# A state-space stage with its group norms, splits, weight copies and convolution banks placed elsewhere

## The chip, the cores and the metric

The kernel runs on one core of one Trainium2 chip. The metric is the device time of one execution in microseconds (us). TensorE (PE) multiplies 128x128 tiles, VectorE (DVE), ScalarE (ACT) and GpSimd (POOL) work element by element, and SyncE (SP) issues the transfers. Each engine runs its own list of instructions strictly in order and waits on semaphores for the others.

## What is computed

A two-layer trunk over 512 rows of 1024 numbers. The change lies in the first layer's mixer, a Mamba-2 state-space layer with four groups of eight heads, cut here to what matters:

```python
proj = h @ w_in
z, xbc, dt = split(proj)
xbc = silu(causal_dwconv(xbc, conv_w, conv_b))     # 4 taps
xs, bm, cm = split(xbc)
y = ssd_scan(xs, bm, cm, dt, dt_bias, a_log)       # two chunks of 256 rows
y = (y + d_skip * xs) * silu(z)
y = rmsnorm(y in 4 groups of 512, norm_g)          # a norm for each group
return y @ w_out
```

## The kernel before

All large products are made from operands that are split into a high and a low part (`split`: ACT copies the high part, DVE subtracts it for the low part), so each 128x128x512 step is three matmuls (`mm3`: lines 153, 154 and 155; `mm3_rows`: lines 387 to 389). Weights come in units of 128x1024 numbers, eight steps each: SP loads a unit into one of four `raw` buffers, and `split_unit` turns it into two of the six `w` buffers, so three units can be ready. `Weights.next` gives out the parts of the current unit in order; `prefetch` loads and splits a unit ahead.

`mamba` goes through four groups g. For each it makes six products (`linear`, 24 matmuls each: the state's B and C, and four of x), each followed by `conv` (one ACT instruction, three on DVE that read the accumulator bank) and a Silu on ACT. Then `ssd` makes the group's scan: it loads the heads' decay exponents (`exponents`: an SP transfer and two POOL additions for each head), and goes through four pairs of heads j: exponentials on ACT (line 824), a product with the shared matrix on DVE (825), matmuls (831, 835, 838), the skip and sum on DVE (843, 845), a gate (`gate`: one more `linear` of 24 matmuls, and a Silu, line 754), a product with it on DVE (847), a square on ACT (849) and its sum over the pairs in `ssq` on DVE (851). At its end comes the group's norm: `rstd` (eight small matmuls, line 319, that sum `ssq` over partitions, a chain of some ten small DVE instructions, lines 297 to 310, and four transposes, line 323), and four DVE multiplications by it (855).

In the code `split_group(g - 1)` follows the scan of group g: four copies on ACT and four subtractions on DVE that make `xo`, the operands of the output projection (`project_out`, which in its first part goes through 16 steps k of 12 matmuls each, with one `mod`, a load and two DVE instructions, in each). In group 0 three of the four gates are made before the scan.

Of the eight PSUM banks two are named `acc`, four `seg` and two `mi`. In groups 1 to 3 the six products and the gates take the two `acc` banks in turn; a bank comes free when the conv's third DVE instruction, or the gate's Silu, has read it. The pool `b4` has 33 buffers of 128x1024 numbers; `h`, `xo`, the exponent tiles, a group's u, xd, y and others all live there.

The order on each engine is fixed when the program is built. A planner takes, for an engine that it believes idle, the ready instruction that stands first in the code; so work that is written later can fill gaps, and where two instructions could run, the one written first does. Buffers of a pool are given out in the same way.

Of the kernel before, what the change touches and what calls it, by code (L numbers as in the profile page):

```python
# [13 lines left out]
AF = mybir.ActivationFunctionType  # L14
OP = mybir.AluOpType
# [9 lines left out]
KI = DI // P  # L25
# [67 lines left out]
class Kernel:  # L93
# [294 lines left out]
        nc.tensor.matmul(ps, x[0][:, ts], wl, start=False, stop=False)  # L388
        nc.tensor.matmul(ps, x[1][:, ts], wh, start=False, stop=stop)  # L389

    def project_out(self, dram, x, x_src, gain, x_dst, first=None, after=None, mods=(), held=()):

        nc = self.nc
        nk = len(x)
        row = self.rows(gain)
        sq = self.small.tile([P, 2, 4], F32, name="sq")
        yg = [None] * 4
# [10 lines left out]
        if first is not None:  # L410
            cols = [1]
            weights = Weights(self, dram)
            pss = first
            for k in range(nk):
                wh, wl = weights.next(4)
                for t in range(4):
                    self.mm3_rows(pss[t], x[k], t, wh, wl, k == 0, k == nk - 1)
                if k < len(mods):
                    self.mod(mods[k])
            for t in range(4):  # L420
                evacuate(pss[t], t, 0)
        xin = self.load_x(x_src)
        held = list(held)
        for i in range(2):
# [25 lines left out]
            for part in ([t] for t in ts) if after is None else [ts]:  # L450
# [3 lines left out]
                rs = self.rsqrt(s, D)  # L454
                for t in part:
                    for cs in [slice(0, D)] if after is not None else [slice(0, 512), slice(512, D)]:
                        nc.vector.scalar_tensor_tensor(out=xin[t][:, cs], in0=yg[t][:, cs], scalar=rs[:, t - lo:t - lo + 1],
                                                       in1=xin[t][:, cs], op0=OP.mult, op1=OP.add)
# [224 lines left out]
    def mamba(self, x, x_src, x_dst):  # L683
        nc = self.nc
        with ExitStack() as es:
            self.keep = es.enter_context(self.tc.tile_pool(name="ssm", bufs=1))
            c = self.constants(CST_M, "cst_m")
            w = Weights(self, self.a["ssm_in"])
            xn = [self.big((P, D)) for _ in range(4)]
            self.unit_rows(x, xn)  # L690
            h = self.pairs(KD)
            scale = self.const.tile([P, KD], F32, name="sc_first")
            pss = self.banks(6)
            for k in range(KD):
# [5 lines left out]
                for n in range(6):  # L700
                    wh, wl = w.next()
                    self.mm3(pss[n], wh, wl, h[k][0], h[k][1], k == 0, k == KD - 1)
            yn, xo = [], []

            def split_group(g):
                for u in yn[g]:
                    m = self.big(dt=F32R)
                    self.split(m[:, 0], m[:, 1], u)
                    xo.append((m[:, 0], m[:, 1]))

            mods = range(16, 24)
            for g in range(4):
# [24 lines left out]
                        zs.append(self.gate(w, h, z[1][:, 0], self.seg()))  # L737
                else:
                    for i in range(6):
                        nc.scalar.activation(u[i], self.conv(self.linear(w, h), tiles[i]), AF.Silu)  # L740
                for j in mods[MODS_SSM[g]:MODS_SSM[g + 1]]:
                    self.mod(j)
                yn.append(self.ssd(g, u[0], u[1], u[2:], w, h, c, zs))
                if g:
                    split_group(g - 1)
            split_group(3)
            gain = self.scale_cols(("post_mix", 0), 16, 0.0)
            h, after = self.before(("pre_ffn", 0), 24)
            self.project_out(self.a["ssm_out"], xo, x_src, gain, x_dst, self.banks(4), after, range(24, 40))
        return h  # L750

    def gate(self, w, h, out, ps=None):
# [14 lines left out]
        nc.gpsimd.tensor_tensor(out=v[:, :, 0], in0=v[:, :, 0], in1=mask, op=OP.add)  # L767
        return e

    def ssd(self, g, bt, ct, xs, w, h, c, zs):  # L770

        nc = self.nc
        es = [self.exponents(8 * g + i, c) for i in range(2)]
# [43 lines left out]
        for j in range(4):  # L817
            mh = []
            now = es
            es = [self.exponents(8 * g + 2 * j + 2 + i, c) for i in range(2)] if j < 3 else []  # L820
            for i, m in enumerate(now):
                hd = 8 * g + 2 * j + i
                for at, n, b in ((0, 256, 0), (256, 256, 2), (512, 128, 1), (640, 128, 3)):
                    nc.scalar.activation(m[:, at:at + n], m[:, at:at + n], AF.Exp, bias=self.nacs[:, b, hd:hd + 1])
                nc.vector.tensor_tensor(out=m, in0=m, in1=cb, op=OP.mult)
                mh.append(m)
# [23 lines left out]
            if j:  # L850
                nc.vector.tensor_tensor(out=ssq, in0=ssq, in1=sq, op=OP.add)
            out.append(y)
        rs = self.rstd(ssq, 512)
        for j in range(4):
            nc.vector.scalar_tensor_tensor(out=out[j], in0=out[j], scalar=self.col("ssm_norm", 4 * g + j), in1=rs,
                                           op0=OP.mult, op1=OP.mult)
        return out


    def rope(self, ps, factor, flat, out):  # L860
# [481 lines left out]
```

## Time and profile before

| | us |
|---|---|
| median of three runs | 1537.9 |
| lowest and highest | 1534.82, 1541.6 |
| the profiled execution | 1535.77 |
| its span, first to last instruction | 1534.0 |

The stretch that the change touches is 86 to 403 us of the span: group 0's scan ends near 121, those of groups 1, 2 and 3 near 192, 273 and 357 us, and the output projection's first part ends at 402. PE's clock has two levels, 2.4 and 1.2 GHz, shown as 1.00 and 0.50 in the column PEclk.

### The profile page before, as it was taken

The page shows a single profiled execution, that of the slowest core. Times are in us where ns is not written, and L with a number is a line of the kernel's source. Part 1 is how long each engine was busy: PE and PEld are TensorE (multiplying, and loading weights), DVE is VectorE, ACT ScalarE, POOL GpSimd, SP SyncE. Part 2 cuts the span into 40 slices and gives each one's busy share as a digit, 9 for nine tenths or more (in the row PEclk, how much of TensorE's full clock was granted, in tenths as well). Part 3 has the DMA queues.
Part 4 walks back from the last instruction along what each step waited for, and adds up shares of the span by engine and source line. Part 5 has one row for each costly group of instructions (what it writes and reads, how often), then busy time and mean ns, then how long its engine had stood idle before and what let it go on. Part 6 is the DMA issues. An engine that isn't in the chain of part 4 may idle for free.

```text
span 1534.0 us, 22547 instructions
## 1 busy us (share of the span) xinstructions
PE 1467.8 (96%) x8514; PEld 1217.7 (79%) x8514; DVE 1112.4 (73%) x1989; ACT 764.8 (50%) x1360; POOL 196.1 (13%) x161
## 2 busy tenths in 40 slices
PE   6999899898999999999999989999999999999997
PEld 4767677676889788888888877777678999999886
DVE  7877676787585788872367588889856878888246
ACT  3574839384363222322257474566644455557143
POOL 0040203040000000000000100000000356661000
PEclk9999999999999999999999999999999999999999
DMA  8443253454763788882466542000043223323254
GB/s 298 164 140 101 65 167 95 151 178 159 261 218 103 270 310 291 294 281 97 163 218 229 125 164 69 15 29 15 15 151 137 70 84 111 109 98 110 97 206 151
DMA packets 70687, 230.47 MB, mean 150 GB/s; under 512 B 8209, under 2 KB 11793, under 8 KB 70578
## 3 DMA queue, kind: packets, MB, share of 16 engines
q1 hardware_dynamic: 70290, 228.77, 44.3%
q8 instruction: 67, 1.10, 0.3%
q14 instruction: 42, 0.34, 0.1%
q10 hardware_dynamic: 288, 0.25, 0.1%
HBM read 215.30 MB, written 8.45 MB: 146 GB/s over the span
## 4 chain that ended last, share of the span: by engine, by line
PE 76%; DVE 13%; DMA 4%; ACT 3%; issue 2%; SPq 1%; POOL 0%; DVEq 0%; ACTq 0%
PE acc L153 12%; PE acc L154 12%; PE acc L155 12%; PE seg L389 5%; PE seg L388 5%; PE seg L387 5%; PE seg L155 3%; PE seg L154 3%; PE seg L153 3%; PE acc L388 3%; PE acc L389 3%; PE acc L387 3%; DVE w L134 2%; PE mi L1190 2%; PE acc L1207 2%
## 5 line engine op out<-in xcount | busy, mean ns | idle before, releaser
L134 DVE TENSOR_TENSOR w<-raw,w 128x1024 fp32r<-128x1024 f32 (+1 forms) x250 | 308.4, 1240 | 180.4 <-ACT w L133 173.3
L133 ACT ACTIVATE w<-raw 128x1024 fp32r<-128x1024 f32 (+1 forms) x250 | 242.2, 971 | 388.0 <-PE seg L388 124.6
L153 PE MATMUL acc<-b,w 128*128 128x512 f32 (+1 forms) x976 | 360.4, 370 | 11.0 <-ACT w L133 6.3
L155 PE MATMUL acc<-b,w 128*128 128x512 f32 (+1 forms) x976 | 356.6, 365 | 0.5 <-DVE w L134 0.5
L154 PE MATMUL acc<-b,w 128*128 128x512 f32 (+1 forms) x976 | 355.4, 364 | 0.5 <-DVE b L134 0.5
L153 PEld LDWEIGHTS acc<-b,w 128*128 128x128 f32 x976 | 186.0, 191 | 42.8 <-ACT w L133 7.0
L155 PEld LDWEIGHTS acc<-b,w 128*128 128x128 f32 x976 | 186.2, 191 | 29.2 <-DVE w L134 1.0
L154 PEld LDWEIGHTS acc<-b,w 128*128 128x128 f32 x976 | 186.2, 191 | 27.6 <-DVE b L134 1.3
L271 DVE SCALAR_TENSOR_TENSOR raw<-raw,b 128x1024 f32<-128x1024 f32 x112 | 136.1, 1221 | 27.5 <-DMA raw<-in_mod_dram 26.8
L388 PE MATMUL seg<-w,b 128*128 128x512 f32 x340 | 133.0, 391 | 0.0
L389 PE MATMUL seg<-w,b 128*128 128x512 f32 x340 | 133.0, 391 | 0.0
L387 PE MATMUL seg<-w,b 128*128 128x512 f32 x340 | 132.7, 391 | 0.0
L867 POOL TENSOR_TENSOR t<-t,b 128x512 f32<-128x512 f32 x12 | 18.0, 1499 | 717.0 <-DVE t L866 714.1
L1158 ACT ACTIVATE b<-seg,nm 128x512 f32<-128x512 f32 (+3 forms) x128 | 65.9, 525 | 64.1 <-DVE nm L1155 63.3
L155 PE MATMUL seg<-b,w 128*128 128x256 f32 (+1 forms) x252 | 77.2, 306 | 1.4 <-DVE w L134 1.4
L154 PE MATMUL seg<-b,w 128*128 128x256 f32 (+1 forms) x252 | 77.1, 306 | 0.0
L153 PE MATMUL seg<-b,w 128*128 128x256 f32 (+1 forms) x252 | 75.6, 306 | 0.0
L389 PEld LDWEIGHTS seg<-w,b 128*128 128x128 f32 x340 | 64.1, 189 | 13.3
L388 PEld LDWEIGHTS seg<-w,b 128*128 128x128 f32 x340 | 64.1, 189 | 13.3
L387 PEld LDWEIGHTS seg<-w,b 128*128 128x128 f32 x340 | 63.8, 188 | 13.0
L133 ACT ACTIVATE b<-t 128x256 fp32r<-128x256 f32 (+1 forms) x94 | 46.3, 516 | 48.9 <-DVE t L539 30.3
L134 DVE TENSOR_TENSOR w<-st,w 128x512 fp32r<-128x512 f32 x68 | 56.9, 841 | 18.6 <-ACT w L133 15.9
(309 smaller groups left out, 2846.4 us busy)
## 6 DMA issues: line engine op xcount, KB each, us to landing
raw<-in_mod_dram SPq DMA_DIRECT2D x112, 512.0 KB, 4.6
raw<-in_ffn_in_dram SPq DMA_DIRECT2D x88, 512.0 KB, 4.2
raw<-in_ffn_out_dram SPq DMA_DIRECT2D x66, 512.0 KB, 3.3
raw<-in_ssm_in_dram SPq DMA_DIRECT2D x41, 512.0 KB, 4.3
raw<-in_ssm_out_dram SPq DMA_DIRECT2D x24, 512.0 KB, 4.2
b<-acsd SPq DMA_DIRECT2D x40, 256.0 KB, 5.2
raw<-in_kv_dram SPq DMA_DIRECT2D x12, 512.0 KB, 4.4
raw<-in_q_dram SPq DMA_DIRECT2D x9, 512.0 KB, 4.6
```

The lines of the kernel that those rows point to most:

```text
L133: nc.scalar.activation(hi, src, AF.Copy)
L134: nc.vector.tensor_tensor(out=lo, in0=src, in1=hi.bitcast(F32), op=OP.subtract)
L153: nc.tensor.matmul(ps, wh, xh, start=start, stop=False, skip_group_check=more)
L154: nc.tensor.matmul(ps, wh, xl, start=False, stop=False, skip_group_check=more)
L155: nc.tensor.matmul(ps, wl, xh, start=False, stop=stop, skip_group_check=more)
L271: i = nc.vector.scalar_tensor_tensor(out=raw, in0=raw, scalar=1.0, in1=self.cs, op0=OP.mult, op1=OP.mult, accum_out=self.modc[:, n:n + 1])
L387: nc.tensor.matmul(ps, x[0][:, ts], wh, start=start, stop=False)
L388: nc.tensor.matmul(ps, x[0][:, ts], wl, start=False, stop=False)
L389: nc.tensor.matmul(ps, x[1][:, ts], wh, start=False, stop=stop)
L1158: nc.scalar.activation(p[o + r], banks[i][:, r * n:(r + 1) * n], AF.Exp, bias=nm[:, o + r:o + r + 1], accum_out=d[:, o + r:o + r + 1])
L1190: nc.tensor.transpose(ps[:, i * n + a * P:i * n + (a + 1) * P], unit["p"][j * per + i][:, a * P:(a + 1) * P], self.ident)
L1207: self.nc.tensor.matmul(po[64 * i:64 * i + 64, bs], vt[a][:, r * 256 + kv * 64:r * 256 + kv * 64 + 64], unit["w"][2 * i + r][:, a * P:(a + ...
```

## The change

- `ssd` no longer ends with its norm. It returns the norm as a function `end`. In groups 1 to 3 the end of group g - 1 is called after the first of group g's six products; that of group 3 is called in `project_out` at step k = 2.
- `split_group` becomes `split_two`. Group g - 1 is split within group g's projections, two tiles after the fifth convolution and two after the sixth; group 3's tiles are split in `project_out` at k = 6. So xo of group g - 1 exists before the scan of group g, and no longer after it.
- In `ssd`, before the exponentials of the last pair (j = 3), three units of weights are asked for: that of the last gate, and two for the next group's first products (none of these two in group 3).
- The six products of groups 1 to 3 go to the four `seg` banks in turn; the gates keep the `acc` banks.

```diff
-    def project_out(self, dram, x, x_src, gain, x_dst, first=None, after=None, mods=(), held=()):
+    def project_out(self, dram, x, x_src, gain, x_dst, first=None, after=None, mods=(), held=(), nk=None, at=None):
-        nk = len(x)
+        nk = nk or len(x)
...
                 wh, wl = weights.next(4)
+                if at is not None and k in at:
+                    at[k]()
                 for t in range(4):
...
-            def split_group(g):
-                for u in yn[g]:
+            def split_two(g, i):
+                for u in yn[g][2 * i:2 * i + 2]:
...
-                        nc.scalar.activation(u[i], self.conv(self.linear(w, h), tiles[i]), AF.Silu)
+                        ps = self.linear(w, h, self.seg())
+                        if i == 0:
+                            ends.pop()()
+                        nc.scalar.activation(u[i], self.conv(ps, tiles[i]), AF.Silu)
+                        if i > 3:
+                            split_two(g - 1, i - 4)
...
-                yn.append(self.ssd(g, u[0], u[1], u[2:], w, h, c, zs))
-                if g:
-                    split_group(g - 1)
-            split_group(3)
+                out, end = self.ssd(g, u[0], u[1], u[2:], w, h, c, zs, 2 if g < 3 else 0)
+                yn.append(out)
+                ends.append(end)
+
+            def last():
+                split_two(3, 0)
+                split_two(3, 1)
...
-            self.project_out(self.a["ssm_out"], xo, x_src, gain, x_dst, self.banks(4), after, range(24, 40))
+            self.project_out(self.a["ssm_out"], xo, x_src, gain, x_dst, self.banks(4), after, range(24, 40), nk=KI,
+                             at={2: ends.pop(), 6: last})
...
+            if j == 3:
+                if not zs[j:]:
+                    w.prefetch()
+                for _ in range(ahead):
+                    w.prefetch()
...
-        rs = self.rstd(ssq, 512)
-        for j in range(4):
-            nc.vector.scalar_tensor_tensor(out=out[j], in0=out[j], scalar=self.col("ssm_norm", 4 * g + j), in1=rs,
-                                           op0=OP.mult, op1=OP.mult)
-        return out
+
+        def end():
+            rs = self.rstd(ssq, 512)
+            for j in range(4):
+                nc.vector.scalar_tensor_tensor(out=out[j], in0=out[j], scalar=self.col("ssm_norm", 4 * g + j), in1=rs,
+                                               op0=OP.mult, op1=OP.mult)
+
+        return out, end
```

## Rows read from the trace of the kernel before

**Rows 1.** The page's first part: busy us, share of the span, instructions.
```profile
PE 1467.8 (96%) x8514; PEld 1217.7 (79%) x8514; DVE 1112.4 (73%) x1989; ACT 764.8 (50%) x1360; POOL 196.1 (13%) x161
```
**Rows 2.** Busy time by stretch: from:to, length, each engine's busy time, PEclk, DMA.
```profile
20.00:40.00 20.00, 20.00 (x84) 15.95 (x83) 18.51 (x42) 5.63 (x8) 0.00 (x0) 1.00 0.90 294
...
99.50:118.40 18.90, 14.64 (x81) 9.06 (x79) 18.54 (x24) 13.44 (x29) 9.89 (x9) 1.00 0.12 42
...
150.00:184.00 34.00, 33.82 (x174) 24.43 (x174) 23.27 (x33) 30.72 (x53) 13.60 (x16) 1.00 0.34 98
184.00:192.00 8.00, 3.92 (x23) 1.90 (x21) 6.57 (x12) 7.25 (x12) 0.00 (x0) 1.00 0.00 0
192.00:198.80 6.80, 6.80 (x20) 5.74 (x21) 4.90 (x14) 0.63 (x1) 0.00 (x0) 0.50 0.57 185
...
208.10:230.40 22.30, 22.19 (x97) 18.09 (x98) 17.02 (x26) 8.88 (x14) 0.00 (x0) 1.00 0.62 196
...
273.90:280.70 6.80, 6.80 (x20) 5.54 (x20) 4.50 (x14) 0.25 (x1) 0.00 (x0) 0.50 0.64 204
...
355.80:362.70 6.90, 5.87 (x18) 5.00 (x19) 5.91 (x14) 1.73 (x2) 0.00 (x0) 0.51 0.46 154
```
**Rows 3.** Timeline of PE: start, us, instruction [idle before <- releaser]; the group ends.
```profile
118.36 0.50 PE L153 MATMUL acc<-b,w 128*128 128x512 f32 x1 [2.31 <-ACT t L754]
...
132.42 0.47 PE L153 MATMUL acc<-b,w 128*128 128x512 f32 x1 [1.23 <-DVE t L617]
...
189.45 0.50 PE L153 MATMUL acc<-b,w 128*128 128x512 f32 x1 [2.30 <-ACT w L133]
191.94 1.84 PE L319 MATMUL mi<-ones,ssq 128*128 128x1 f32 x8 [1.75 <-DVE ssq L851]
...
208.13 0.47 PE L153 MATMUL acc<-b,w 128*128 128x512 f32 x1 [0.87 <-ACT w L133]
...
273.45 1.46 PE L319 MATMUL mi<-ones,ssq 128*128 128x1 f32 x8 [1.76 <-DVE ssq L851]
...
354.41 0.73 PE L387 MATMUL acc<-w,b 128*128 128x512 f32 x2 [2.37 <-ACT w L133]
356.83 1.86 PE L319 MATMUL mi<-ones,ssq 128*128 128x1 f32 x8 [1.23 <-DVE ssq L851]
```
**Rows 4.** Timeline of all engines, 184 to 202 us, ACT and DVE lines.
```profile
184.49 1.28 ACT L754 ACT_TABLE_LOAD   x1
...
186.28 2.17 ACT L133 ACTIVATE b<-b 128x512 fp32r<-128x512 f32 x4
...
188.35 1.04 ACT L133 ACTIVATE w<-raw 128x1024 fp32r<-128x1024 f32 x1
...
191.80 1.22 DVE L134 TENSOR_TENSOR w<-raw,w 128x1024 fp32r<-128x1024 f32 x1
...
200.90 2.72 DVE L855 SCALAR_TENSOR_TENSOR b<-b,vec,mi 128x512 f32<-128x512 f32 x4 [2.93 <-PE mi L323]
```
**Rows 5.** DVE by line, 189.45 to 230.4 us (group 2's projections): count, busy.
```profile
L617 DVE SCALAR_TENSOR_TENSOR t<-acc,vec,t 128x511 f32<-128x511 f32 (+2 forms) x15 | 11.2, 745 | 0.2
L134 DVE TENSOR_TENSOR w<-raw,w 128x1024 fp32r<-128x1024 f32 x8 | 9.8, 1221 | 4.2 <-ACT w L133 4.2
L271 DVE SCALAR_TENSOR_TENSOR raw<-raw,b 128x1024 f32<-128x1024 f32 x4 | 4.9, 1220 | 0.0
```
**Rows 6.** Timelines of SP, POOL and PE: exponent tiles in groups 1 and 3.
```profile
162.88 2.02 SPq L762 DMA_DIRECT2D b<-acsd  x4
...
326.83 1.48 SPq L762 DMA_DIRECT2D b<-acsd  x3
...
337.13 0.33 SPq L762 DMA_DIRECT2D b<-acsd  x1
...
340.29 1.54 POOL L765 TENSOR_TENSOR b<-b,b 128x256 f32<-128x256 f32 x1 [3.11 <-DMA b<-acsd]
341.79 1.17 POOL L767 TENSOR_TENSOR b<-b,b 128x256 f32<-128x256 f32 x1
...
343.83 0.43 PE L831 MATMUL mi<-b,b 128*64 128x256 f32 x1 [0.29 <-DVE b L825]
...
350.53 0.43 PE L831 MATMUL mi<-b,b 128*64 128x256 f32 x1 [0.79 <-DVE b L825]
```

More of the change, by code (lines that the diff above doesn't have):

```diff
@@ L702, in mamba @@
                     self.mm3(pss[n], wh, wl, h[k][0], h[k][1], k == 0, k == KD - 1)
-            yn, xo = [], []
-            def split_group(g):
-                for u in yn[g]:
+            yn, xo, ends = [], [], []
+            def split_two(g, i):
+                for u in yn[g][2 * i:2 * i + 2]:
                     m = self.big(dt=F32R)
@@ L768, in exponents, with ssd @@
         return e
-    def ssd(self, g, bt, ct, xs, w, h, c, zs):
+    def ssd(self, g, bt, ct, xs, w, h, c, zs, ahead):
         nc = self.nc
```

## The prediction

> **What bounds the kernel now.** I read the page's busy shares first: PE is busy 96% of the span, the next engine, DVE, 73% [rows 1]. So time can only be gained where PE stands still or runs slowly. The table by stretches shows where that is. In the projections (208 to 230 us) 97 matmuls start in 22.3 us, one in 0.23 us, without a pause at clock 1.00; in the scan of group 1 (150 to 184 us) PE is busy 33.8 of 34 us, with the gates filling the waits. At the end of the group, 184 to 192 us, it is busy 3.9 of 8 us, and then 6.8 us run at clock 0.50 [rows 2]. The slow stretch comes again after group 2 (273.9 us) and after group 3 (355.8 us) [rows 2]. No other engine is the limit there: DVE works 23.3 and ACT 30.7 of the scan's 34 us [rows 2].
>
> The PE timeline names the waits [rows 3]. After group 1 PE waits 2.30 us for a weight copy, does two matmuls, waits 1.75 us for `ssq`, and later 0.87 us. The last is put down to a weight copy, but the first product's bank was still being read by its conv, so I take it as a bank wait. The end of group 2 repeats these three gaps to 0.01 us. After group 0 there are two waits, 2.31 us for a gate's Silu and 1.23 us for a conv, both for a bank. After group 3 there are 2.37 us for a weight copy and 1.23 us for `ssq`.
>
> ACT and DVE show why the weights are late [rows 4]. ACT first makes the four copies of `split_group` (2.17 us from 186.28), and only at 188.35 the copy of the next product's weights; DVE's low part follows at 191.80. The copies stand earlier in the code, and both are ready.
>
> **The change part by part.**
>
> *Weights ahead of the last heads, splits moved.* Nothing is added: two weight units (ACT 1.04 us, DVE 1.22 us each) and the eight split instructions change places [rows 4]. With two units ready PE has 48 matmuls, 48 x 0.23 = 11.0 us, to run at the moment the gates are done. The 2.30 us go at the ends of groups 1 and 2. The price: up to 2 x 1.04 us of ACT and 2 x 1.22 us of DVE stand ahead of the last pair's exponentials, so `ssq` comes 0 to 4.5 us later. I take about 2, since ACT is nearly full there (30.7 of 34 us) while DVE has gaps. This is hidden by the 11.0 us of products. In group 3 no unit is asked for ahead; only the 2.17 us of copies leave ACT's queue, so its copy for the output projection starts about 2 us earlier, but the second matmul still needs DVE's low part, which competes with the last `ssq` steps. Bounds 0 and 2.37 us; I take 0.9.
>
> *The norm among the projections.* PE's eight `rstd` matmuls now stand in the code behind 24 matmuls of the first product (5.5 us), so the 1.75 us (groups 1, 2) and 1.23 us (group 3, behind two steps of 12 matmuls) find other work. If the planner sets `rstd` too early by its own reckoning, PE stops in front of it again; bounds 0 and 1.75 us at each of three ends, and I take 0.5, as a first product's worth of time lies between. On DVE the small chain and four multiplications (2.72 us) now stand ahead of the first conv. DVE waits there for the transposes, 2.93 us before [rows 4], and behind it are conv and the low parts of weights. PE feels that only when its 11.0 us of ready products and the free banks are used up.
>
> *Four banks.* The conv waits, 1.23 us after group 0 and 0.87 us after groups 1 and 2, and the 2.31 us for the gate's bank after group 0, go: the first products no longer share banks with gates, and a third and fourth product can start before the first conv is read. DVE's demand bounds this. In group 2's projections it does 11.2 us of conv, 9.8 of weights, 4.9 of `mod` and 2.7 of norm [rows 4, 5], 28.6 in 41 us. Six products without pauses last 6 x 24 x 0.23 = 33 us, and the moved splits bring about as much as their copies on ACT, 2.2 us: 31 of 33. DVE would be nearly full, and some of its work would slide into the scan, where it has 10.7 us free [rows 2]. So I cost it at nothing, and at 1 to 3 us a group if that cover is gone.
>
> *The clock.* The three stretches of 6.8 us at 0.50 each do half the work: 3.4 us lost each, 10.2 in all. All three begin after two waits close together with few matmuls between [rows 2, 3]. After group 0 there is one wait of 2.31 us, and no such stretch. With both waits gone I expect all three stretches to go.
>
> *Buffers.* The split tiles of group g - 1 (4 buffers) now live through the scan of group g in place of its 2 y buffers. In group 3 that fills `b4`: 10 for constants, c and `h`, 12 of xo, 7 of the group's u, `ea`, `cb` and xd, 1 y, leave 3 of 33 for exponent tiles; before, 10 + 10 + 7 + 1 left 5. The rows bear the count out: group 1 asks for four tiles at once, group 3 gets three and the last only at 337.13, 10.3 us after [rows 6]. With 3, the second tile of each pair waits for the pair before. From its transfer to the end of its POOL part took 337.13 to 342.96, 5.8 us [rows 6]; with about 2.7 us for its exponentials and product some 8.5 us, against a spacing of 6.7 us between the last two pairs' matmuls (343.83 and 350.53) [rows 6]. So 0 to 2 us for each of the last pairs, 0 to 5 in all; xo of three groups is there by then, so output projection steps can fill in. I take 1.
>
> *The sum*, against the profiled execution (1535.77 us; span 1534.0, the rest lies around it): group 0: 2.31 + 1.23 = 3.5. Groups 1 and 2: 2.30 + 1.75 + 0.87 + 3.4 = 8.3 each, less 0.5 = 7.8. Group 3: 0.9 + 1.23 + 3.4 - 0.5 = 5.0, less 1 for buffers = 4.0. In all 3.5 + 15.6 + 4.0 = 23.1. Part of group 0's other pauses may be filled too: PE is busy 14.6 of 18.9 us there, 4.3 us idle of which 2.3 are counted [rows 2]; I take 1 of the 2. So 24 us: 1535.8 - 24 = 1511.8. The median of the runs shown is 2.1 us above the profiled execution, so 1514.
>
> **The rivals.**
>
> *The clock does not come back, or falls elsewhere.* A remaining wait of some 2 us at each end may be enough for a slow stretch. For: only one end without a slow stretch is seen, and the pauses' places shift. Against: group 0's 2.31 us. Time: the 10.2 us are not gained, 1524. The Trainium skill ("TensorE: Matmul & The Clock Gate", "A second HAM failure mode: psum-queue depth-cycling") has a rule that speaks against four banks: going through PSUM banks in turn made the clock swing in one kernel. By it a swing in each of three projections would cost the same 10.2 us. The trace does not agree: 20 to 40 us goes round six banks at 1.00 [rows 2].
>
> *The buffers cost group 3 its gain.* The last pair comes 5 us late, and PE has nothing to fill it, as the copies of the output weights stand behind the pair on ACT. Group 3's 4.0 are lost and 0 to 5 more: 1518 to 1523; with one slow stretch more, 1526.
>
> *The planner leaves things as they are.* The weight copies are put behind the exponentials again, and only bank waits go (3.5 + 2 x 0.87 = 5.2): 1533. For: before, free buffers and loaded weights did not bring them ahead. Against: they now stand ahead in the code.
>
> *Slower.* The full pool makes group 3's exponent tiles come one by one, because other tiles take what is free. Each pair then costs 8.5 us and another 2 to 3 for the second tile's POOL and ACT part, and 2 for its matmuls, some 13 in place of 6.7: 6.3 x 3 = 19 us, and each stop can bring a slow stretch, 10.2 more. With the 4.0 not gained: 1514 + 33 = 1547. It decides where fewer than two tiles are free through the scan and PE finds no other work there. Against: the 12 xo are ready, 12 steps of other work.
>
> **How the numbers follow.** Forecast (15 to 33 us gained, 1505 to 1523, the low end with all of group 0's pauses and the DVE, `ssq` and buffer costs at nothing) 0.59. Clock 0.16. Buffers 0.09. Planner 0.10. Slower 0.06. The likeliest is 1514. From 1504 to 1528 lie the forecast, the clock and nearly all of the buffers, some 0.82; planner and slower are left out. A measurement of this kernel can tell about 0.5% (7.7 us) from no change: below 1530.2 lie the first three, 0.83; the planner's case with a little more is "same", 0.11; slower 0.06.
>
> **What would show it.** In the trace after: no wait of over 1 us for a weight copy or `ssq` at the group ends; clock 1.00 from 86 to 380 us; weight copies on ACT before the last exponentials; DVE above 90% in the projections; the `rstd` of groups 1 and 2 some 73 us apart in place of 81.5 (191.94 to 273.45 [rows 3]). Wrong would be: PE gaps in front of line 319, products waiting for convs, exponent tiles of group 3 after the pair before, or a slow stretch that stays.

## The result, and the profile after

| | before | after |
|---|---|---|
| median of 4 runs each, us (lowest to highest) | 1536.44 (1534.82 to 1541.6) | 1512.88 (1507.09 to 1518.51) |
| ratio, 95% interval | | 0.983 (0.9807 to 0.9853) |
| profiled execution, us; its span | 1535.77; 1534.0 | 1507.09; 1505.3 |

The change gains 23.6 us by the medians; 24 were forecast. The two profiled executions differ by more, 28.7 us of span. The profiled execution of after is the lowest of its four. The mean granted clock of these four runs goes from 0.993 to 0.996, and the trace of before has a stretch at half clock at 939.5 us, where the change touches nothing, that this execution of after lacks. So sizes of a few us are read below from the state-space stage alone, not from whole spans.

To measure the stage I take two marks that every kernel has: the start of group 0's first scan matrix on PE (line 784 in before) and the start of the first square of the output projection on ACT (line 403). **M** is the time between. Before it is 402.8 - 79.9 = 322.9 us, after 375.4 - 80.9 = 294.5, 28.4 less. By group, the first view is the busy times from one group's first scan matrix to the next's, in the kernel before (columns: from:to, length, busy time of PE, PEld, DVE, ACT and POOL with their instructions, PEclk, DMA share, GB/s):

```profile
79.90:148.80 68.90, 62.19 (x305) 46.40 (x305) 50.85 (x75) 39.44 (x68) 15.43 (x16) 1.00 0.36 118
148.80:230.40 81.60, 76.39 (x356) 57.80 (x356) 58.91 (x93) 51.42 (x81) 13.60 (x16) 0.96 0.40 123
230.40:311.90 81.50, 76.27 (x356) 57.66 (x355) 58.93 (x94) 51.35 (x81) 13.63 (x16) 0.96 0.39 123
311.90:402.80 90.90, 85.24 (x404) 66.01 (x403) 71.08 (x121) 50.71 (x79) 16.86 (x17) 0.96 0.58 187
```

The same four stretches in after, then four short ones in it: the places that answer to the slow stretches of [rows 2], and the second half of group 2's projections:

```profile
80.90:143.30 62.40, 61.53 (x305) 46.43 (x304) 47.77 (x74) 37.60 (x68) 15.44 (x16) 1.00 0.41 129
143.30:216.10 72.80, 72.57 (x355) 55.91 (x354) 58.43 (x93) 50.82 (x80) 15.06 (x16) 1.00 0.42 130
216.10:289.70 73.60, 73.10 (x355) 55.69 (x354) 56.82 (x93) 51.55 (x81) 13.80 (x16) 1.00 0.42 131
289.70:375.40 85.70, 83.04 (x403) 63.97 (x402) 69.12 (x123) 48.74 (x78) 14.76 (x17) 1.00 0.65 209
...
192.00:198.80 6.80, 6.80 (x35) 5.74 (x35) 5.83 (x14) 2.05 (x3) 0.00 (x0) 1.00 0.61 208
198.80:216.10 17.30, 17.30 (x80) 14.33 (x79) 17.09 (x33) 7.30 (x11) 0.00 (x0) 1.00 0.50 159
266.30:273.10 6.80, 6.80 (x35) 5.76 (x34) 6.60 (x18) 2.48 (x3) 0.00 (x0) 1.00 0.66 219
339.70:346.60 6.90, 6.90 (x35) 5.86 (x35) 6.13 (x19) 1.06 (x1) 0.00 (x0) 1.00 0.79 259
```

The lengths shrink by 6.5, 8.8, 7.9 and 5.2 us, with the same matmuls to within one. Take length less PE's busy time: PE stood still for 6.71, 5.21, 5.23 and 5.66 us before, and for 0.87, 0.23, 0.50 and 2.66 after. The granted clock was 1.00 throughout. The places of the slow stretches (20, 20 and 18 matmuls at 0.50, [rows 2]) now hold 35 matmuls each.

Two numbers thus explain M. **Idle**: before 22.8 us, after 4.3, a gain of 18.5. **Clock**: half of PE's busy time in stretches at 0.50 (1.2 GHz in place of 2.4), before (6.80 + 6.80 + 5.87) / 2 = 9.7 us, after none. Together 28.2 of the 28.4 measured.

The PE timeline of after, from 100 to 376 us, has no wait of [rows 3] left. These are the only two waits over 0.7 us, and two lines of the norm:

```profile
192.28 0.95 PE L319 MATMUL mi<-ones,ssq 128*128 128x1 f32 x8
203.64 0.60 PE L323 MATMUL mi<-ident,y 128*128 128x128 f32 x4
...
304.38 0.43 PE L849 MATMUL mi<-b,b 128*64 128x256 f32 x1 [1.03 <-DVE b L843]
324.36 0.43 PE L849 MATMUL mi<-b,b 128*64 128x256 f32 x1 [1.63 <-DVE b L843]
```

`rstd` of group 1 (line 319) has no idle time before it and takes 0.95 us, not 1.84. Its transposes (line 323) come 11.4 us after it, because the small chain between them takes turns on DVE with the convs (DVE was busy 17.09 of 17.30 us, the window above), and nobody waits for that. The two waits that are left lie in group 3's scan. ACT in after, group 1's end and group 3, against [rows 4]:

```profile
175.98 1.05 ACT L133 ACTIVATE w<-raw 128x1024 fp32r<-128x1024 f32 x1
178.76 1.04 ACT L133 ACTIVATE w<-raw 128x1024 fp32r<-128x1024 f32 x1
184.92 1.05 ACT L133 ACTIVATE w<-raw 128x1024 fp32r<-128x1024 f32 x1
...
316.07 1.05 ACT L133 ACTIVATE w<-raw 128x1024 fp32r<-128x1024 f32 x1
320.30 0.40 ACT L842 ACTIVATE b<-b,nacs 128x128 f32<-128x128 f32 x1 [3.18 <-POOL b L777]
```

At the end of group 1 the weight copies run from 175.98 on, where the first stood at 188.35. The line at 316.07 is a copy for the output projection, made in the middle of group 3's scan. It stands in ACT's idle time before the late exponentials at 320.30. Those are late because of the exponent tiles, which SP and POOL show, against [rows 6]:

```profile
296.41 6.25 SPq L774 DMA_DIRECT2D b<-acsd  x2
...
305.99 0.32 SPq L774 DMA_DIRECT2D b<-acsd  x1
315.76 1.28 SPq L774 DMA_DIRECT2D b<-acsd  x3
319.49 0.78 POOL L777 TENSOR_TENSOR b<-b,b 128x256 f32<-128x256 f32 x1 [6.12 <-PE mi L849]
```

The second pair's two tiles are asked for over 6.25 us, not together; then one at 305.99 and the last three only at 315.76, both times right after the matmuls of a pair. So the pool was short of buffers in this scan, as the prediction counted.

### The profile page after: what moved, and what is told of

The parts are those of the page before. It is cut to its first block, busy times and chain, and to the rows that moved or that the text cites. A ratio compares the mean times of both kernels' runs of the same rounds, so it can differ in the third digit from the quotient of the medians.

```text
span 1505.3 us, 22518 instructions
## 1 busy us (share of the span) xinstructions
PE 1457.6 (97%) x8514; PEld 1211.0 (80%) x8514; DVE 1106.1 (73%) x1989; ACT 762.5 (51%) x1358; POOL 195.9 (13%) x161
## 4 chain that ended last, share of the span: by engine, by line
PE 77%; DVE 13%; DMA 4%; ACT 3%; issue 2%; SPq 0%; POOL 0%; DVEq 0%; ACTq 0%; POOLq 0%
PE acc L153 10%; PE acc L154 10%; PE acc L155 10%; PE seg L155 5%; PE seg L154 5%; PE seg L153 5%; PE seg L387 5%; PE seg L389 5%; PE seg L388 5%; PE acc L388 3%; PE acc L389 3%; PE acc L387 3%; DVE w L134 2%; PE mi L1211 2%; PE acc L1228 1%
## 5 line engine op out<-in xcount | busy, mean ns | idle before, releaser
L153 PE MATMUL acc<-b,w 128*128 128x512 f32 (+1 forms) x832 | 300.0, 362 | 1.6 <-ACT b L133 1.2
L155 PE MATMUL acc<-b,w 128*128 128x512 f32 (+1 forms) x832 | 297.7, 358 | 0.5 <-DVE w L134 0.5
L154 PE MATMUL acc<-b,w 128*128 128x512 f32 (+1 forms) x832 | 297.4, 357 | 0.2 <-DVE b L134 0.2
L153 PEld LDWEIGHTS acc<-b,w 128*128 128x128 f32 x832 | 157.2, 190 | 25.1 <-ACT b L133 2.3
L155 PEld LDWEIGHTS acc<-b,w 128*128 128x128 f32 x832 | 157.6, 189 | 24.1 <-issue 1.5
L154 PEld LDWEIGHTS acc<-b,w 128*128 128x128 f32 x832 | 157.8, 190 | 21.7 <-DVE b L134 1.3
L155 PE MATMUL seg<-b,w 128*128 128x256 f32 (+1 forms) x396 | 134.1, 339 | 1.4 <-DVE w L134 1.4
L154 PE MATMUL seg<-b,w 128*128 128x256 f32 (+1 forms) x396 | 134.3, 339 | 0.0
L153 PE MATMUL seg<-b,w 128*128 128x256 f32 (+1 forms) x396 | 133.2, 340 | 0.0
L155 PEld LDWEIGHTS seg<-b,w 128*128 128x128 f32 x396 | 75.7, 191 | 10.3 <-DVE w L134 2.2
L154 PEld LDWEIGHTS seg<-b,w 128*128 128x128 f32 x396 | 75.8, 191 | 7.9 <-issue 0.3
L153 PEld LDWEIGHTS seg<-b,w 128*128 128x128 f32 x396 | 75.8, 191 | 7.7 <-issue 0.2
L389 PEld LDWEIGHTS seg<-w,b 128*128 128x128 f32 x340 | 63.8, 188 | 13.2
L387 PEld LDWEIGHTS seg<-w,b 128*128 128x128 f32 x340 | 63.9, 188 | 13.0
```

The lines of the kernel that those rows point to most:

```text
L153: nc.tensor.matmul(ps, wh, xh, start=start, stop=False, skip_group_check=more)
L154: nc.tensor.matmul(ps, wh, xl, start=False, stop=False, skip_group_check=more)
L155: nc.tensor.matmul(ps, wl, xh, start=False, stop=stop, skip_group_check=more)
L387: nc.tensor.matmul(ps, x[0][:, ts], wh, start=start, stop=False)
```

## The experiments

Each kernel's whole time was compared with runs of before on the same chip (medians of before there: 1539.75 to 1540.93). Idle and clock are read in each trace from the same views as above; the last column is M less both. It stays between 288.5 and 292.7 in every kernel but the one that adds matmuls, so nearly every difference in M is idle time or clock.

M is read from one execution of each kernel, and it has a spread of its own. The scan of group 0 has the same code in after, e3, e4, e8, e11 and e12, yet PE stands still in that group's stretch for 0.87 us in after and for 0.86 to 2.4 us in the others, all of it inside this scan. Two of these stretches, e3 and e11 (columns as above):

```profile
81.31:145.38 64.07, 61.69 (x305) 46.43 (x304) 49.81 (x75) 39.17 (x69) 15.42 (x16) 1.00 0.38 126
81.58:145.53 63.95, 61.66 (x306) 46.44 (x304) 49.80 (x75) 39.17 (x69) 15.45 (x16) 1.00 0.39 127
```

So up to 1.7 us of a difference in M against after can lie there and say nothing of the part that was changed. The expectations of e1 to e7 and e9 name the start of the first square itself, 402.8 us before and 375.4 after; it is given beside M.

| kernel | median, us | ratio (95%) | M | idle | clock | rest |
|---|---|---|---|---|---|---|
| before | 1536.44 | 1 | 322.9 | 22.8 | 9.7 | 290.4 |
| after | 1512.88 | 0.983 (0.9807 to 0.9853) | 294.5 | 4.3 | 0 | 290.2 |
| e1_two_banks | 1525.12 | 0.9908 (0.9891 to 0.9926) | 308.9 | 13.1 | 4.7 | 291.1 |
| e2_no_ahead | 1522.87 | 0.9889 (0.9871 to 0.9907) | 304.5 | 12.5 | 0 | 292.0 |
| e3_norm_at_end | 1513.89 | 0.9831 (0.9816 to 0.9847) | 296.5 | 6.1 | 0 | 290.4 |
| e4_splits_behind_scan | 1519.99 | 0.9876 (0.9854 to 0.9899) | 301.7 | 11.1 | 0 | 290.6 |
| e5_only_banks | 1532.27 | 0.9954 (0.9935 to 0.9973) | 313.6 | 16.9 | 8.2 | 288.5 |
| e6_only_ahead | 1526.5 | 0.9928 (0.9901 to 0.9955) | 308.9 | 16.0 | 3.0 | 289.9 |
| e7_norm_and_splits | 1536.99 | 0.9982 (0.9962 to 1.0002) | 319.7 | 22.0 | 5.0 | 292.7 |
| e9_filler | 1532.27 | 0.9963 (0.9945 to 0.9982) | 318.4 | 10.2 | 3.4 | 304.8 |
| e8_late_splits | 1517.75 | 0.9852 (0.9828 to 0.9875) | 296.4 | 5.8 | 0 | 290.6 |
| e10_gate_request_only | 1519.76 | 0.9877 (0.9858 to 0.9895) | 305.1 | 11.8 | 1.7 | 291.6 |
| e11_late_splits_k4 | 1514.52 | 0.9848 (0.982 to 0.9875) | 298.9 | 6.9 | 1.5 | 290.5 |
| e12_out_weights_ahead | 1510.18 | 0.9814 (0.9788 to 0.984) | 293.6 | 3.4 | 0 | 290.2 |

My theory is that waits at the group ends, and the half clock that they bring, were all that was lost, and that ready products take their place. The rivals: one part does it all; the clock follows something else than the waits; the buffers of group 3 cost what the rest gains. The first four kernels take one part out of the change.

**e1_two_banks**

```diff
-                        ps = self.linear(w, h, self.seg())
+                        ps = self.linear(w, h)
```

> The changed kernel with its convolutions back on the two acc banks. Measure: the start of the first square of the output projection (402.8 us in the trace before, 375.4 after). My theory: the bank waits come back, 3.5 us after group 0 and 0.9 after groups 1 and 2, about 5 us: 380.5. Rival (the banks do nothing once weights come ahead): 375.4 within 1 us. Rival (the banks are the main part, because a product made ahead has nowhere to go without them): over 12 us lost, 388 or later, with slow stretches of the clock.

M grew by 14.4 us (first square at 389.6), and half of the whole gain went. That is the second rival, with its slow stretches, and not the 5 us of the theory. The PE timeline of e1, one wait, and what DVE did before it:

```profile
278.59 0.76 PE L153 MATMUL acc<-b,w 128*128 128x512 f32 x1 [4.06 <-DVE t L304]
```

```profile
274.31 0.74 DVE L619 SCALAR_TENSOR_TENSOR t<-acc,vec,t 128x511 f32<-128x511 f32 x1
274.96 0.16 DVE L299 TENSOR_SCALAR y<-v 128x4 int32<-128x4 int32 x1
275.03 1.22 DVE L134 TENSOR_TENSOR w<-raw,w 128x1024 fp32r<-128x1024 f32 x1
...
276.24 0.75 DVE L619 SCALAR_TENSOR_TENSOR t<-acc,vec,t 128x510 f32<-128x510 f32 x1
...
277.70 0.75 DVE L619 SCALAR_TENSOR_TENSOR t<-acc,vec,t 128x509 f32<-128x509 f32 x1
```

A conv is three instructions of 0.75 us, but here the first product's conv takes from 274.31 to 278.44, 4.1 us: the norm's small steps, a weight's low part and the second product's conv (276.97, among the lines left out) lie between. Both banks are held, so products that have their weights can't be made. A stretch of 6.8 us at 0.50 begins in this wait, at 277.8; after group 0 the wait of 2.31 us for the gate's Silu is back, with 3.4 us at 0.50. Idle and clock account for 13.5 of the 14.4 us. The banks are not an edit beside the others: they are what lets the deferred norm and the weights made ahead do their part.

**e2_no_ahead**

```diff
-            if j == 3:
-                if not zs[j:]:
-                    w.prefetch()
-                for _ in range(ahead):
-                    w.prefetch()
```

> The changed kernel without the three requests for weights before the last pair. My theory: the copies of the splits no longer stand in front, so the weights come some 2 us earlier than before by that alone, and the loss is small, 0 to 2 us at each of two ends: 375.4 to 379. Rival (the requests are what fills the group's end): the 2.3 us waits come back with the slow stretches, 2 x (2.3 + 3.4) = 11 us: 387.

M grew by 10.0 us, none of it by the clock (first square at 385.2). The size is near the rival's, but the waits for weights and the slow stretches of which the rival was made did not come. PE and ACT of e2 at the end of group 1:

```profile
182.29 0.65 PE L844 MATMUL mi<-b,b 128*64 128x256 f32 x2 [2.07 <-DVE b L838]
185.23 0.50 PE L153 MATMUL seg<-b,w 128*128 128x512 f32 x1 [0.21 <-ACT w L133]
```

```profile
184.12 2.94 ACT L133 ACTIVATE w<-raw 128x1024 fp32r<-128x1024 f32 x3
```

The copies come only behind the last gate's Silu, as before. But the wait for them is now 0.21 us, since the copies of the splits no longer stand ahead of them in ACT's queue. The loss sits earlier than I had it: PE waits 2.07 us inside the last pair, for the product of its exponentials, where in after the next group's first product fills in, from 179.19 us on.

**e3_norm_at_end**

```diff
-                        if i == 0:
-                            ends.pop()()
...
-                ends.append(end)
+                end()
```

> The changed kernel with each group's norm written at the end of its scan again, the splits, weights and banks as changed. My theory: PE may still run the products made ready ahead in the time, but the planner sets the sums of squares in front of them by its own reckoning, so waits of 1 to 1.75 us at three ends come back, 3 to 5 us, without slow stretches: 379 to 381. Rival (a wait for ssq is what slows the clock): 3.4 us more at each end, 389.

M grew by 2.0 us (idle by 1.8; first square at 377.8, earlier than both expectations); in the whole time, 1.0 us in the median, it cannot be told from after. With ready products at each end the planner finds other work before `rstd` even where it stands in the code at the old place. After group 1 nothing is waited for there:

```profile
194.60 0.95 PE L319 MATMUL mi<-ones,ssq 128*128 128x1 f32 x8
```

Of the 2.0 us 1.7 lie in group 0's stretch, as in e11, and only 0.3 in the three other groups. So within the change the norm's move is not shown to gain anything.

**e4_splits_behind_scan**

```diff
-                        if i > 3:
-                            split_two(g - 1, i - 4)
...
+                if g:
+                    split_two(g - 1, 0)
+                    split_two(g - 1, 1)
```

> The changed kernel with the splits of group g - 1 behind the scan of group g again; norm, weights and banks as changed. My theory: with two units ready the 2.2 us of copies cost PE nothing, and group 3's scan has 5 buffers for exponent tiles in place of 3, so its two waits (1.3 and 1.8 us) go: 372.5 to 375. Rival (moving the splits is what brought the weights forward): 2 us lost at each end, 381. In group 3 the copies stand again in front of the output weights, which may cost 1 to 2 us there.

M grew by 7.2 us (first square at 381.7, where the rival had it, though not 2 us at each end), 5.1 of it in group 3 (90.8 in place of 85.7), 1.4 in group 0's stretch. PE and ACT of e4 there:

```profile
332.94 0.43 PE L850 MATMUL mi<-b,b 128*64 128x256 f32 x1 [1.34 <-DVE b L844]
...
336.66 0.73 PE L387 MATMUL acc<-w,b 128*128 128x512 f32 x2 [0.72 <-ACT w L133]
...
339.17 0.50 PE L388 MATMUL acc<-w,b 128*128 128x512 f32 x1 [1.31 <-DVE w L134]
```

```profile
332.85 2.18 ACT L133 ACTIVATE b<-b 128x512 fp32r<-128x512 f32 x4
...
335.56 1.05 ACT L133 ACTIVATE w<-raw 128x1024 fp32r<-128x1024 f32 x1
```

The output projection's first weights are copied at 335.56, behind the four split copies, and PE waits for them and for their low part (0.72 and 1.31 us), besides waits in the last two pairs that nothing fills (1.24, 0.93, 1.34). In after that copy ran at 316.07 and the output projection's steps filled the last pair from 328.20 on. So the moved splits are worth 5.1 us in group 3, not the 0.9 of the prediction, and some 6 to 7 us in all.

The next kernels put one part into the kernel before, and one fills the pauses alone.

**e5_only_banks**

```diff
-                        nc.scalar.activation(u[i], self.conv(self.linear(w, h), tiles[i]), AF.Silu)
+                        nc.scalar.activation(u[i], self.conv(self.linear(w, h, self.seg()), tiles[i]), AF.Silu)
```

> The kernel before with the one change that the convolutions of groups 1 to 3 take the four seg banks. Measure: the start of the first square of the output projection (402.8 us before, 375.4 after). Prediction's step: only the bank waits go, 3.5 after group 0 and 0.9 after groups 1 and 2: 397.5. Rival (banks are the main part by themselves, as leaving them out of the change cost 14 us): 389 or earlier. Third: the two waits for weights and ssq at the ends of groups 1 and 2 stay with their slow stretches in any case, since nothing here brings the weights forward; so not under 395.

M fell by 9.3 us; idle and clock account for 7.4. The first square, at 397.2, stands where the step had it (397.5), but by luck: this execution has a slow stretch at 43.0 us, ahead of the change, and its first scan matrix starts at 83.6 in place of 79.9. So the banks alone gave more than the step allowed, and less than the rival. The two waits of group 1's end, and the three places behind the group ends:

```profile
188.53 0.50 PE L153 MATMUL seg<-b,w 128*128 128x512 f32 x1 [2.29 <-ACT w L133]
191.03 1.87 PE L319 MATMUL mi<-ones,ssq 128*128 128x1 f32 x8 [1.76 <-DVE ssq L851]
```

```profile
189.80:196.60 6.80, 5.57 (x17) 4.80 (x18) 5.77 (x14) 1.92 (x3) 0.00 (x0) 0.50 0.42 134
268.30:275.10 6.80, 5.23 (x17) 4.12 (x16) 5.93 (x11) 2.52 (x3) 0.00 (x0) 0.50 0.32 96
350.20:357.00 6.80, 5.68 (x17) 4.84 (x18) 5.81 (x14) 1.82 (x2) 0.00 (x0) 0.50 0.41 136
```

The waits of 2.29 and 1.76 us stay, and so does each slow stretch. The largest part of what the banks bring alone comes in group 0 (4.6 us by its length).

**e6_only_ahead** (the block taken out in e2, put into before)

```diff
+            if j == 3:
+                if not zs[j:]:
+                    w.prefetch()
+                for _ in range(ahead):
+                    w.prefetch()
```

> The kernel before with only the requests for weights ahead of the last pair. Prediction's step: the 2.3 us waits at the ends of groups 1 and 2 go, and with one wait of two left the clock stays up: 402.8 - 2 x 5.7 = 391.4. Rival (two acc banks: the product made ahead has no bank until the last gate's Silu and the first conv have read theirs): the wait only changes its name, and under 4 us are gained: 399 or later.

M fell by 14.0 us (first square at 389.1, the step had 391.4), more than any other single part gives. The places behind the three group ends:

```profile
192.00:198.80 6.80, 6.80 (x35) 5.76 (x34) 6.14 (x13) 2.58 (x4) 0.00 (x0) 1.00 0.12 44
273.90:280.70 6.80, 6.37 (x28) 5.34 (x29) 6.80 (x16) 3.36 (x5) 0.00 (x0) 1.00 0.65 204
342.30:349.10 6.80, 5.95 (x18) 5.09 (x19) 5.80 (x14) 1.54 (x2) 0.00 (x0) 0.50 0.48 154
```

Groups 1 and 2, which have weights ahead, keep 1.00, and not only the wait for the weight copy is gone there but also that for `ssq` (`rstd` at 193.83 and 270.45, without idle time before it): ready weights fill both.

Group 3, for which nothing is asked ahead, keeps its waits (2.37 and 1.22 us) and its slow stretch.

**e7_norm_and_splits** (after, with the edits of e1 and e2)

```diff
-                        ps = self.linear(w, h, self.seg())
+                        ps = self.linear(w, h)
...
-            if j == 3:
-                if not zs[j:]:
-                    w.prefetch()
-                for _ in range(ahead):
-                    w.prefetch()
```

> The changed kernel with the convolutions on two banks and without the requests for weights: what is left is the norm among the next projections and the splits moved. Theory: the 2.2 us of copies and the ssq wait leave the group's end, so both waits after groups 1 and 2 shrink to under 1.5 us and the slow stretches go: 385 to 389. Rival (without a bank and without weights nothing can run there): waits for a bank of 2 to 4 us, slow stretches at some ends: 392 to 398.

M fell by 3.2 us, and the whole time can't be told from before's (first square at 399.6, later than both expectations). The ends lose their waits for the weight copy and for `ssq`, and their slow stretches, but idle hardly moves (22.8 to 22.0). DVE does the norm's four multiplications (2.71 us from 205.90) and parts of `mod` among the convs, and the two banks stay held:

```profile
212.99 0.47 PE L153 MATMUL acc<-b,w 128*128 128x512 f32 x1 [3.12 <-DVE t L619]
```

Behind this wait, and one like it at 295.43, lie 3.4 us at 0.50. So with two banks the norm's move does what the prediction named as its danger: products waiting for convs. With four banks (after, e2) no such wait is seen.

**e9_filler** (before, with six unread matmuls at each end of groups 1 to 3; nothing else is changed)

```diff
+        if g:
+            idle = self.seg()
+            for i in range(6):
+                nc.tensor.matmul(idle, self.ident, mh[i % 2][:, 0:512], start=True, stop=True)
```

> The kernel before with six matmuls of 128x512 in groups 1 to 3, written at the scan's end, whose result nobody reads; five of them run between the last pair's matmuls and the next product, where PE stood idle, and nothing that PE waits for comes earlier. Theory (the slow stretches follow from the pauses, and cost 3.4 us each): clock 1.00 through the ends, waits as before or filled, 402.8 - 10.2 + 0 to 2 = 392.6 to 395. Rival (the slow stretches come from something else, or the work that follows was limited by DVE and ACT there in any case): 402 to 405, or no slow stretch and no gain.

Three group ends and a place behind group 0 in e9:

```profile
186.00:200.00 14.00, 13.99 (x62) 8.99 (x62) 11.34 (x25) 7.57 (x11) 0.00 (x0) 1.00 0.30 85
266.00:280.00 14.00, 14.00 (x62) 9.01 (x62) 11.28 (x24) 7.40 (x10) 0.00 (x0) 1.00 0.28 88
346.00:362.00 16.00, 16.00 (x73) 10.26 (x72) 12.91 (x29) 9.88 (x16) 0.31 (x1) 1.00 0.32 106
118.50:125.30 6.80, 6.80 (x22) 5.65 (x21) 3.92 (x13) 1.93 (x3) 0.00 (x0) 0.50 0.14 55
```

The first weight copy of group 1's end starts at 190.06 us. The `rstd` behind it:

```profile
195.39 0.95 PE L319 MATMUL mi<-ones,ssq 128*128 128x1 f32 x8
```

Counted from the group's first scan matrix (150.5) these two come 39.6 and 44.9 us later; in the kernel before it is 39.6 and 43.1. All three ends stay at 1.00, though the weights and `ssq` come no earlier than before. So the half clock there comes from PE's pauses, not from what it waits for. Idle and clock fall by 12.6 and 6.3 us, but the rest rises by 14.4, 4.8 for each end's six matmuls, so that only 4.5 are left. The theory left this out, and the first square, at 399.4, lies between the two expectations. (The 3.4 us of clock that e9 still loses are one stretch after group 0, which before does not have behind the same wait of 2.31 us.) Filling with useful work is what the change adds to that.

Two questions were left: why e2 lost inside the last pair, and what the late exponent tiles cost.

**e10_gate_request_only**

```diff
-                out, end = self.ssd(g, u[0], u[1], u[2:], w, h, c, zs, 2 if g < 3 else 0)
+                out, end = self.ssd(g, u[0], u[1], u[2:], w, h, c, zs, 0)
```

> The changed kernel that asks ahead only for the last gate's weights, not for the next group's two units. By the same measure (294.5 after, 304.5 with none of the three requests). Theory (the two units of the next group are what fills the group's end): 301 to 305. Rival (the 2 us wait in the last pair came from the last gate's weights): 295 to 297.

M is 305.1, within 0.6 us of e2, as the theory had it (1.7 of it are a slow stretch that e2 lacks). Its trace has e2's wait inside group 1's last pair again (2.08 us). So asking early for the gate's own weights brings nothing that shows, and the next group's two units are what fills the end.

**e8_late_splits** and **e11_late_splits_k4** free the split tiles of group 2 during group 3's scan: its splits go into the output projection, at step 0 and at step 4.

```diff
-                        if i > 3:
+                        if i > 3 and g < 3:
...
+            def late():
+                split_two(2, 0)
+                split_two(2, 1)
...
-                             at={2: ends.pop(), 6: last})
+                             at={0: late, 2: ends.pop(), 6: last})
```

> The changed kernel, but group 2's four tiles are split in the output projection at k = 0 and not before group 3's scan, so that scan has 2 more buffers. Measure: the start of the first square of the output projection less the start of the first scan matrix (294.5 us in the trace after, 322.9 before). Theory (the full pool makes group 3's exponent tiles late): the two waits of 1.3 and 1.8 us go, 291 to 293, and SP asks for the tiles of a pair together. Rival (what counts is that the copies are out of the way of the output weights, as the run with all splits behind the scan lost 5 us in this stage): 297 to 300.

> As the run with group 2's tiles split in the output projection, but at k = 4, behind group 3's norm. By the same measure: if the pool is what costs time in group 3, 291 to 293, and 1 to 2 us less than with k = 0 if the copies still stood in front of the output weights there; if the pool costs nothing, 294.5 or more.

The tiles now come earlier: e8 asks for three at 306.36, where after asked for one at 305.99 and three at 315.76. Yet M rose, by 1.9 us in e8, all of it in group 3, and by 4.4 in e11, 2.7 of it in group 3 (1.5 of these a slow stretch) and 1.6 in group 0, whose code is the same. So the theory of both failed, though in the whole time neither can be told from after. PE of e11 in the last pair, and its ACT:

```profile
330.78 0.65 PE L853 MATMUL mi<-b,b 128*64 128x256 f32 x2 [0.93 <-DVE b L847]
333.39 0.69 PE L853 MATMUL mi<-b,b 128*64 128x256 f32 x1 [1.34 <-DVE b L847]
```

```profile
333.31 1.05 ACT L133 ACTIVATE w<-raw 128x1024 fp32r<-128x1024 f32 x1
```

The waits move into the last pair, and the first copy for the output projection comes at 333.31, not at 316.07: ACT no longer has the idle time in which it was made. The late tiles cost two waits (1.03 and 1.63 us) and paid for them with an early copy. What the last pair seems to lack is other ready work.

**e12_out_weights_ahead** tests that: e11, with two units of the output projection's weights asked for ahead of group 3's last pair.

```diff
+            wo = Weights(self, self.a["ssm_out"])
...
-                out, end = self.ssd(g, u[0], u[1], u[2:], w, h, c, zs, 2 if g < 3 else 0)
+                out, end = self.ssd(g, u[0], u[1], u[2:], w, h, c, zs, w if g < 3 else wo)
...
-                             at={2: ends.pop(), 6: last})
+                             at={2: ends.pop(), 4: late, 6: last}, ws=wo)
...
-                for _ in range(ahead):
-                    w.prefetch()
+                for _ in range(2):
+                    ahead.prefetch()
```

> The kernel with group 2's tiles split at k = 4 of the output projection, and with two units of the output projection's weights asked for ahead of group 3's last pair, as the other groups do for their followers. In the changed kernel the first of these copies stood at 316.1 us, in an idle time of ACT that a late exponent tile had made; with the tiles split late it stood at 333.3 and PE waited 1.1 and 1.6 us (1.09 and 1.60 from start to start) for the last pair with nothing else ready. Measure: first square less first scan matrix (294.5 after, 298.9 with the splits at k = 4, of which 1.7 a slow stretch). Theory (what PE lacks in the last pair is ready output weights, not buffers): PE fills these waits, 292 to 294.5. Rival (the two copies ahead of the last exponentials only push the pair back): 297 or later.

From 295 us to the end of the stage PE of e12 has one wait with a releaser left:

```profile
319.79 0.43 PE L854 MATMUL mi<-b,b 128*64 128x256 f32 x1 [0.26 <-DVE b L848]
```

This is the theory's range. Its group 3 takes 83.2 us in place of 85.7 in after, with 0.4 us idle, so ready weights do fill the last pair. No run asks for these weights with the splits left in place, so what the freed tiles add to it is not shown. M is 5.3 us under e11's, and 0.9 under after's: e12 has 1.2 us more idle time in group 0 (2.04 in place of 0.87), where its code is the same. Its whole time, 1510.18, can't be told from after's: the intervals overlap.

## Why the prediction was right, and where its terms were not

**The time and the main reason hold.** The sum had 23.1 + 1 us. In the stage's marks 28.4 went, by the medians 23.6. That the medians agree with the forecast to 0.4 us is partly luck, since the stage's own gain, in the two profiled executions, is 4.4 larger. By group 4.5, 7.8, 7.8 and 4.0 were forecast; 6.5, 8.8, 7.9 and 5.2 were measured. The waits and the slow stretches of [rows 3] and [rows 2] are gone, as the list of what would show it asks: no wait for a weight copy or `ssq` is left, clock 1.00 from 86 to 380 us; copies ahead of the last exponentials; DVE at 99% in group 2's projections; `rstd` of groups 1 and 2 at 192.28 and 266.3, 74.0 us apart in place of 81.5, where 73 was forecast.

**The clock's term**, 10.2, was 9.7 by busy time. e9 shows that the pauses bring it, e5 that it stays while both waits stay, e6 that it goes with the weights. So the rival in which it stays or falls elsewhere failed. The Trainium skill ("TensorE: Matmul & The Clock Gate", "A second HAM failure mode: psum-queue depth-cycling") tells of a kernel that went through PSUM banks in turn and whose PE idled for short times between groups of products, often enough that the clock swung. The prediction took from it the turn through the banks alone. After goes round four banks in three projections at 1.00, with PE at work all the time (the windows above): the turn alone made no swing here, and the idling between products was not there to test.

**The parts were mis-sized, and the total came near because several terms count the same idle time.** The step that failed first is the four banks' term, 5.2 us: they gave 7.4 to 9.3 alone and 14.4 within the change. The prediction said that a third and fourth product can start before the first conv is read, and its sum has no term for that. e1 and e7 show its price: with two banks the deferred norm turns into waits of 3 to 4 us for a conv, with slow stretches behind them. The second is the moved splits in group 3, 0.9 us within bounds of 0 and 2.37: 5.1 there within the change (e4), because the bound was taken from the first wait alone and not from what the copies hold up in the last pair, and also at the other ends (e2: 0.21 us for a copy where 2.30 stood). The norm's term, 1.75 x 2 + 1.23 - 1.5 = 3.2, was at most 2.0 within the change, and 0.3 outside group 0's stretch (e3): in groups 1 and 2 the weights made ahead fill the wait for `ssq` by themselves (e6). The weights' 2.30 x 2 with the clock of two ends, 6.8, make 11.4; 14.0 alone and 10.0 within the change were measured. But e2 shows that within the change they fill the last pair rather than take away the 2.30 us.

Parts in before add up to 9.3 + 14.0 + 3.2 = 26.5, parts taken out (e1 to e4) to 33.6, the whole is 28.4. So none of them can be given a share of its own.

**Group 0's pauses**: 1 of 2 us was taken; idle fell by 5.8, 3.5 of it the two bank waits, so all of the 2 came in this execution; in others with the same scan up to 1.5 less did, so that is partly luck. **DVE's cover held**: nearly full, the norm's chain stretched over 11 us, and no wait of PE in the projections came of it. **The price of weights ahead** was taken too low: the last step of group 1's `ssq` starts at 191.23, 47.9 us after the group's first scan matrix, and before at 191.20, 42.4 after it. These 5.5 us are more than the 0 to 4.5 allowed, but the ready products hid them, as the prediction said.

**Buffers**: the mechanism was right: fewer free tiles, and the later ones asked for only after a pair's matmuls. Its cost, taken as 1 us within 0 to 5, is 2.66 us of waits, of which nothing is gained by freeing the tiles (e8, e11) until other work is ready too (e12, 2.5 us in group 3). The rival that loses all of group 3's gain to it failed on the words "as the copies of the output weights stand behind the pair": they ran at 316.07. The slower rival's condition was met in part (a pair's tiles asked for one by one), but other work was there: 2.66 us of waits, none with a slow stretch behind it. The planner's rival failed: the copies moved from 188.35 to 175.98.

What stays open: 1.9 of e5's 9.3 us and 2.3 us of e7, which are neither idle time nor clock in their traces (the rest of 288.5 and 292.7 in the table), and why PE waits 0.9 us in group 0's scan in some executions and over 2 in others with the same code there.

## What to carry to other kernels

Where PE waits at the end of a stage, ask what other work is ready, and count all that it needs: a product made ahead wants its weights split and a bank that nobody holds, and either alone brings only a part. A wait of the full engine costs again when the clock falls behind it (here 3.4 us behind waits of 2.30 and 1.75), so the whole group end is priced, not the wait alone. And before a small difference is put down to a part, look whether it lies where the part was changed. Before a full pool is relieved, look at what the late tile lets happen in its place, here a weight copy in ACT's idle time.

## What was not expected of the hardware

Every slow stretch inside M, in all fourteen traces, lies in or behind a pause of PE of over 1.2 us. But the same pause brought the half clock in one kernel and not in another. Behind the wait of 2.31 us after group 0 there is no slow stretch in before and e6, 3.4 us in e1 and e7, and 6.8 us in e9. Waits of 0.93 and 1.34 us in the last pair were followed by 3.4 us at 0.50 in e11 and by none in e8; a wait of 2.07 us in e2 by none, and one of 1.63 us in e10 by 3.4 us. Two waits of 2.29 to 2.37 and 1.22 to 1.76 us close together brought it every time that they were seen (before, e5, e6). A single pause of this size can't be priced from one trace; only an end without pauses was safe in all of these runs.
